# A two-layer attention and SwiGLU trunk on one core: another start of the attention phase, and other numbers in its planner

## The chip, the core and the metric

The kernel runs on one core of a Trainium2 chip. The metric is the device time of one execution in microseconds (us). TensorE (PE) multiplies, VectorE (DVE), ScalarE (ACT) and GpSimd (POOL) do the rest, and SyncE (SP) issues most transfers.

## The reference, cut to what matters

Two layers; in each a mixing part and a SwiGLU part, both with a norm before and after. All is float32, with 512 tokens of 1024 features, head size 64, 4 differential heads and 8 forgetting (fox) heads.

```python
cos, sin = rotary_tables(positions, x.dtype)      # 8 frequencies
for l in range(DEPTH):
    h = rms_norm(x, attn_pre_g[l])
    qa, ka, va, qb, kb, vb, f_logit = jnp.split(h @ w_in[l], split_at, axis=-1)
    qa = partial_rotary(qa, cos, sin)             # first quarter of each head
    ka = partial_rotary(ka, cos, sin)
    oa = diff_attention(qa, ka, va, lam)          # softmax 1 - lam * softmax 2, times va
    oa = rms_norm(oa, diff_sub_g[l]) * (1.0 - lam_init)
    log_f = jax.nn.log_sigmoid(f_logit + forget_bias[l])
    ob = forgetting_attention(qb, kb, vb, log_f)  # logits plus c_i - c_k, c = cumsum(log_f)
    x = x + rms_norm(jnp.concatenate([oa, ob], -1) @ w_out[l], attn_post_g[l])
    h = rms_norm(x, ffn_pre_g[l])
    y = (jax.nn.silu(h @ w_gate[l]) * (h @ w_up[l])) @ w_down[l]
    x = x + rms_norm(y, ffn_post_g[l])
```

## The kernel before, in words

**Exactness.** Every float32 matrix is split into a high part in TensorE's rounded float32 format (`A.copy`, ScalarE) and the rest (`tensor_sub`, VectorE or GpSimd), and a product takes three matmuls: high by high, high by low, low by high. So each weight chunk of 512 KB costs a transfer on SP's queue, a cast and a subtraction ahead of its 24 matmuls. `load_w` (L247) does this for the feed-forward part, `load` (L629) for the attention part. There are two raw buffers ("wr") and three pairs of split ones ("w").

**Stages.** Layer 0's attention runs from 0 to about 268 us, its feed-forward part to 584 and its down projection and the next norm to 644, layer 1's attention to about 876 us, and the rest to the end at 1231. The feed-forward products run in the plain order of the program, and the framework places what is not pinned. Instructions that are pinned keep the order of the program on their engine.

**The attention phase is planned.** `Plan` (L71) is a list scheduler that runs while the program is built. Every step is an `Op` with an engine, an estimated duration, its dependencies, a key (lower goes first), buffers that it takes and gives back, and a latency until its result can be used (for transfers the flight). `run` (L98) keeps one clock for each engine and for SP's queue and picks what can start first, by key among those that are ready. The order that it finds is pinned on each engine. The chip's own times do not matter any more then: each engine is in order, and an operation that comes later than planned holds up all behind it on its engine. Projections have the key `FILLER` (1e6): they go wherever TensorE has nothing else, in the fixed sequence `FILL = "d0 d1 d2 v1 d3 f0 v0 f1 f2 f3"`, and then the first part of the output projection (`o0_chunk`, L1090, columns 0 to 511 of w_out, and `o1_chunks`). Durations stand in `dV`, `dA` and `dG` (a fixed part and one for each column), and some are written at the place.

**A head.** A diff projection ("pj_kd", "pj_qd", `tile_chunk`, L670) gives a tile in PSUM. VectorE makes the rotary part: `t1` = tile * cosT, `pair` shuffles into `t2`, `t2` *= sinT (L739), `t1` += `t2`. `stack` splits the result by halves; for a key, SP copies each half to the other 64 partitions (`dup`, L714). Scores (`score`, L853) go to PSUM, VectorE adds the mask or the fox bias and takes the maximum (L875), ScalarE takes the exponential with its sum (L886). Diff heads then combine two rows ("ed", L958), fox heads scale one ("ae", L1037). TensorE transposes them, ScalarE and VectorE split them ("pth", "ptl", L919 and L923), and TensorE multiplies with V. GpSimd makes the fox bias ("ae", L1020 and L1022) from "cb", a row of sums that SP spreads over the partitions, and, in this kernel, the low parts of most weight chunks (L649).

**The start** (`start`, L397, layer 0 alone). x, the identity and four chunks of the diff V weights are loaded in turn, tokens are normalised by tiles of 128, transposed by TensorE ("hp_a") and split (L497, L502), and V is made tile by tile ("va"). Until then TensorE does empty products ("va<-sinT"). Raw V weights lie in `mixed_d` and `raw_v`, their split parts in the tiles of queries and keys. The rotary tables are made in `tables` (L525): eight transfers of positions, a chain of small VectorE steps (L554 to L572) behind the weights, three sines, a store to DRAM and four loads into cosT and sinT.

**The first gate chunks.** `gate` and `up` (L1229, L1232) call `proj_T` (L320). Its matmuls are pinned while `pinned[0]` holds, the splits of its weights are not.

Of the kernel before, what the change touches and what calls it, by code (L numbers as in the profile page):

```python
# [35 lines left out]
TB = S // 16  # L36
VA_C, VA_T = 4, 1
# [7 lines left out]
C_ID, C_M, C_F, NKEEP, C_U = 0, 128, 640, 641, 641  # L45
# [16 lines left out]
class Op:  # L62
    def __init__(self, eng, dur, fn, deps, key, take, give, lat):
        self.eng, self.dur, self.fn, self.key, self.take, self.give, self.lat = eng, dur, fn, key, take, give, lat
        self.users, self.after, self.left, self.ready, self.end = [], [], 0, 0.0, None
        for d in deps:
            d.users.append(self)
            self.left += 1


class Plan:  # L71


    def __init__(self, slots, margin):
        self.free = {k: [0.0] * n for k, n in slots.items()}
        self.margin, self.ops, self.last, self.idle = margin, [], {}, None

    def add(self, eng, dur, fn, deps=(), key=0.0, take=(), give=(), lat=0.0, order="", ready=0.0):
        o = Op(eng, dur, fn, deps, key, take, give, lat)
# [18 lines left out]
    def run(self, pin, first):  # L98
        clock = dict.fromkeys("VAGQ", 0.0)
        clock["P"] = first  # L100
        cands = {e: [o for o in self.ops if o.eng == e and not o.left] for e in clock}
        todo = len(self.ops)
        while todo:
            best = None
            for e, c in cands.items():
                opts = []
                for o in c:
                    s = self.slots_at(o)
                    if s is not None:
                        r = max(s, o.ready)  # L110
                        opts.append((max(r, clock[e]), o.key, r, o))
# [12 lines left out]
            clock[o.eng] = start + o.dur  # L124
            o.end = start + o.dur + o.lat
# [34 lines left out]
def _constants():  # L160
# [6 lines left out]
    c[:, C_M + S - P:C_M + S] = np.where(r[None, :] > r[:, None], np.float32(-BIG), np.float32(0.0))  # L167
    expo = np.arange(0, ROT, 2, dtype=np.float32) / np.float32(ROT)
    inv_freq = (np.float32(1.0) / np.power(np.float32(500000.0), expo).astype(np.float32)).astype(np.float32)
    c[:, C_F] = inv_freq[r // 16]  # L170
    return c
# [3 lines left out]
def hymba_block(ctx, tc, x_d, pos_d, apre_d, win_d, fb_d, lq1_d, lk1_d, lq2_d, lk2_d, dsg_d, wout_d, apost_d,  # L175
# [64 lines left out]
    V.memset(sinT, 0.0)  # L240
    G.memset(cosT, 1.0)
# [5 lines left out]
    def load_w(src, shape, name, eng=None, dst=None, raw=None):  # L247
# [10 lines left out]
        A.copy(hi, raw)  # L258
        (eng or V).tensor_sub(lo, raw, hi.bitcast(F32))  # L259
# [60 lines left out]
    def proj_T(src_w, col, name):  # L320

        wh, wl = load_w(src_w[:, col:col + P].rearrange("(k p) n -> p k n", p=P), [P, KT, P], name)
# [24 lines left out]
    for l in range(DEPTH):  # L347
        win = win_d[l]
        with ExitStack() as actx:
# [12 lines left out]
            mixed_d = ap.tile([P, NDIFF, S], F32, name=f"mixd{l}", tag="v8", bufs=5)  # L362
            if l == 0:
                raw_v = ap.tile([P, NDIFF, S], F32, name=f"rawv{l}", tag="v8", bufs=5)
# [18 lines left out]
            vd, tab = [], []  # L383
# [12 lines left out]

            def start():  # L397

                plan.free.update(g=[], v8=[0.0], qs=[], ks=[])
# [9 lines left out]
                idd = dma(con[:, :P], con_d[:, :P], P)  # L409

                def w_load(c):
                    raw = (mixed_d, raw_v)[c // 2][:, 2 * (c % 2):2 * (c % 2) + 2]
                    if c == 0:
                        dst = q_tile("wva0h"), q_tile("wva0l")
                    elif c < 3:
                        w = k_tile(f"wva{c}")
                        dst = w[:, 0], w[:, 1]
                    else:
                        dst = [wpool.tile([P, WCH], F32R, name=f"{x}_va3", tag=x).rearrange("p (a b) -> p a b", a=2)
                               for x in ("wh", "wl")]  # L420
                    hi, lo = dst
                    d = dma(raw, win[2 * c * P:(2 * c + 2) * P, VA:VA + S].rearrange("(k p) n -> p k n", p=P), 2 * S)
                    ops = []
                    for k in range(2):
                        wva[2 * c + k] = hi[:, k], lo[:, k]
                        a = add("A", dA(S), lambda k=k: A.copy(hi[:, k], raw[:, k]), [d], key=-85 + c,
                                take=["w"] if c == 3 and k == 0 else [], order="hi w" if c == 3 and k == 0 else "")
# [13 lines left out]
                zeros = sinT.bitcast(mybir.dt.bfloat16)  # L441
# [16 lines left out]
                for t in range(NT):  # L458
# [24 lines left out]
                    for z in range(2):  # L483
# [20 lines left out]
                        p = add("P", 436, tr, [v, idd], key=key, take=["ts"[z]], give=["e"])  # L504
# [3 lines left out]
                for t in range(NT):  # L508
                    for c in range(4):
                        def vas(t=t, c=c):  # L510
                            if t == NT - 1:
# [4 lines left out]
                                         key=500 + VA_C * c + VA_T * t)  # L516
                    vd_split(t, [done[t, 3]])
                for c in range(4):
                    add("P", 0, lambda: None, [done[t, c] for t in range(NT)], key=-99,
                        give=(["qs", "qs"], ["ks"], ["ks"], ["w"])[c])  # L520
                add("P", 0, lambda: None, wl[2] + wl[3], key=-99, give=["v8"])
                add("P", 0, first_va.clear, [done[t, 0] for t in range(NT)], key=-99)
                return hT[NT - 1, 1]

            def tables(last):  # L525

# [3 lines left out]
                tab_d = dpool.tile([4, 8, S], F32, name="tab_d", tag="tabd")  # L530
# [4 lines left out]
                def get(dst, src, n, **kw):  # L535
                    return add("Q", max(400, 1.43 * n), lambda: nc.sync.dma_start(dst(), src), key=1, lat=2000,
                               order="ld" + "".join(f" {k}" for k in kw.get("take", ())), **kw)

                def positions():
                    w = rbuf("rd", F32, "rot")  # L540
                    x["p"] = w[:, :TB].bitcast(I32)
# [901 lines left out]
```

## Time and profile before

| what | value |
| --- | --- |
| median of 3 runs | 1233.08 us (1230.33 to 1235.37) |
| the profiled execution's own time | 1233.1 us |
| its span, first to last instruction | 1231.3 us |
| busy: PE, DVE, ACT, POOL | 1195.3, 816.5, 597.1, 214.1 us |
| mean granted TensorE clock | 0.996 |

The span is the time that the trace shows; the execution's own time is 1.8 us longer. A matmul counts as busy from its start to its modelled end, so bare time of PE is the least that is lost. A name such as `t2kd<-t2kd,sinT` gives the tile that is written and those that are read.

### The profile page before, as it was taken

The numbers are of one execution on the slowest core, as the hardware profiler recorded it, in microseconds if no ns is written. First come the engines' busy times: TensorE is split into PE (matmuls) and PEld (weight loads), VectorE is DVE, ScalarE is ACT, GpSimd is POOL, SyncE is SP. The second block draws the span as 40 slices with busy tenths as digits, with TensorE's granted clock in tenths as the row PEclk, the third lists the DMA queues.
The fourth block names the chain that finished last, engine by engine and source line by source line (L and its number), as shares of the span: only waits on it lengthen the run. The fifth ranks groups of instructions, "written<-read, shape, count | busy, mean of one in ns | idle before, by whom it ended". The sixth has DMA issues, their size and how long they took to land.

```text
span 1231.3 us, 16721 instructions
## 1 busy us (share of the span) xinstructions
PE 1195.3 (97%) x5817; PEld 987.0 (80%) x5817; DVE 816.5 (66%) x1574; ACT 597.1 (48%) x1158; POOL 214.1 (17%) x250
## 2 busy tenths in 40 slices
PE   8998999999999999999999999999999999999997
PEld 5787877788888888888777878777988888888886
DVE  7698858765554555577848987695656455455776
ACT  5476657553332323365644767674533332333643
POOL 1302457320000000000223124672200000000010
PEclk9999999999999999999999999999999999999999
DMA  7333433416576676798513333433167667677964
GB/s 234 88 91 88 119 99 110 151 35 195 182 235 197 210 229 192 234 321 297 187 32 98 95 91 97 124 104 118 52 201 225 206 202 237 182 238 239 312 231 137
DMA packets 211268, 206.75 MB, mean 168 GB/s; under 512 B 11680, under 2 KB 155680, under 8 KB 211184
## 3 DMA queue, kind: packets, MB, share of 16 engines
q1 hardware_dynamic: 211040, 205.16, 53.5%
q8 instruction: 46, 0.75, 0.2%
q10 hardware_dynamic: 144, 0.52, 0.1%
q14 instruction: 38, 0.31, 0.1%
HBM read 163.34 MB, written 33.91 MB: 160 GB/s over the span
## 4 chain that ended last, share of the span: by engine, by line
PE 76%; DVE 11%; issue 7%; ACT 3%; POOL 2%; DMA 1%; POOLq 0%; DVEq 0%; SPq 0%; ACTq 0%
PE pj_g L205 20%; PE pj_u L205 19%; PE o L205 5%; PE da L205 5%; PE dc L205 5%; PE va L205 3%; PE pj_kd L205 3%; PE pj_kf L205 2%; PE db L205 2%; PE pj_qf L205 2%; PE vb L205 1%; DVE t2kd L739 1%; PE of L205 1%; PE pj_qd L205 1%; PE ptf L210 1%
## 5 line engine op out<-in xcount | busy, mean ns | idle before, releaser
L205 PE MATMUL pj_g<-hT_h,wh_g 128*128 128x512 f32 (+1 forms) x384 | 142.9, 372 | 0.0
L205 PE MATMUL pj_g<-hT_h,wl_g 128*128 128x512 f32 (+1 forms) x384 | 142.6, 371 | 0.0
L205 PE MATMUL pj_g<-hT_l,wh_g 128*128 128x512 f32 (+1 forms) x384 | 142.6, 371 | 0.0
L205 PE MATMUL pj_u<-hT_h,wh_u 128*128 128x512 f32 (+1 forms) x368 | 140.1, 381 | 0.0
L205 PE MATMUL pj_u<-hT_l,wh_u 128*128 128x512 f32 (+1 forms) x368 | 139.8, 380 | 0.0
L205 PE MATMUL pj_u<-hT_h,wl_u 128*128 128x512 f32 (+1 forms) x368 | 139.7, 380 | 0.0
L271 POOL TENSOR_SCALAR v_fp<-s_fp 128x1 f32<-128x1 f32 x8 | 7.6, 946 | 664.4 <-DVE c L1369 625.1
L259 DVE TENSOR_TENSOR wl_u<-wr_u,wh_u 128x1024 fp32r<-128x1024 f32 x44 | 53.9, 1225 | 99.6 <-ACT wh_u L258 99.6
L258 ACT CAST wh_g<-wr_g 128x1024 fp32r<-128x1024 f32 x44 | 46.4, 1054 | 146.3 <-PE pj_u L205 99.0
L258 ACT CAST wh_u<-wr_u 128x1024 fp32r<-128x1024 f32 x44 | 46.3, 1053 | 135.5 <-PE pj_g L205 128.3
L1239 DVE TENSOR_TENSOR sg<-pj_u,sg 128x512 f32<-128x512 f32 x44 | 30.4, 691 | 84.6 <-PE pj_u L205 84.6
L205 PE MATMUL da<-wh_d,op 128*128 128x512 f32 x264 | 82.6, 390 | 0.0
L205 PEld LDWEIGHTS pj_g<-hT_h,wh_g 128*128 128x128 f32 x384 | 72.3, 188 | 12.5
L205 PEld LDWEIGHTS pj_g<-hT_l,wh_g 128*128 128x128 f32 x384 | 72.3, 188 | 12.6
L205 PEld LDWEIGHTS pj_g<-hT_h,wl_g 128*128 128x128 f32 x384 | 72.3, 188 | 12.5
L205 PEld LDWEIGHTS pj_u<-hT_l,wh_u 128*128 128x128 f32 x368 | 69.2, 188 | 13.1
L205 PEld LDWEIGHTS pj_u<-hT_h,wl_u 128*128 128x128 f32 x368 | 69.2, 188 | 13.1
L205 PEld LDWEIGHTS pj_u<-hT_h,wh_u 128*128 128x128 f32 x368 | 69.2, 188 | 13.0
L258 ACT CAST wh_d<-wr_d 128x1024 fp32r<-128x1024 f32 x42 | 44.2, 1053 | 43.6 <-PE da L205 8.9
L259 DVE TENSOR_TENSOR wl_d<-wr_d,wh_d 128x1024 fp32r<-128x1024 f32 x42 | 51.3, 1221 | 17.7 <-ACT wh_d L258 17.5
L258 ACT CAST wh_d<-xr 128x1024 fp32r<-128x1024 f32 (+1 forms) x42 | 38.1, 908 | 43.7 <-PE da L205 13.2
L205 PEld LDWEIGHTS da<-wh_d,op 128*128 128x128 f32 x264 | 49.6, 188 | 10.2
(298 smaller groups left out, 3085.4 us busy)
## 6 DMA issues: line engine op xcount, KB each, us to landing
wr_g<-in_w_gate_dram SPq DMA_DIRECT2D x44, 512.0 KB, 4.6
wr_u<-in_w_up_dram SPq DMA_DIRECT2D x44, 512.0 KB, 4.6
b<-in_w_down_dram SPq DMA_DIRECT2D x88, 256.0 KB, 3.3
t_d<-b SPq DMA_DIRECT2D x88, 256.0 KB, 4.2
wr_d<-t_d SPq DMA_DIRECT2D x24, 512.0 KB, 4.6
wr_d<-in_w_down_dram SPq DMA_DIRECT2D x18, 512.0 KB, 5.0
wr_o<-in_w_out_dram SPq DMA_DIRECT2D x16, 512.0 KB, 4.4
xr<-t_d SPq DMA_DIRECT2D x16, 512.0 KB, 4.8
```

Source lines behind the costliest of these rows:

```text
L205: ins = PE.matmul(out, a, b, start=start, stop=stop)
L210: ins = PE.transpose(out, a, idn)
L258: A.copy(hi, raw)
L259: (eng or V).tensor_sub(lo, raw, hi.bitcast(F32))
L271: G.tensor_scalar(v, s2[:, 0:1], scalar1=s2[:, 1:2], scalar2=EPS, op0=ALU.add, op1=ALU.add)
L739: return V.tensor_mul(b["t2"], b["t2"], sinT)
L1239: V.tensor_mul(sg, pu, sg)
```

## The change

The start is another one. Raw V weights lie in the buffers of the probabilities ("pt"), their split parts in three tiles of "v8" and one pair of "w"; `mixed_d` is taken later (`mix`). The rotary tables are made at the very start (`rotary`): ScalarE loads the trigonometric table set and issues one transfer of the positions, with tokens on partitions; VectorE multiplies by eight constants and reduces the angle; ScalarE puts the sines into two zero or one tiles; TensorE transposes these in eight steps and ScalarE copies them to cosT and sinT. V products of token tiles 2 and 3 get a key behind the first diff projections, whose key goes ahead of other fillers. `Op` has a flag `port`: a flagged VectorE step does not start in the plan before the last GpSimd step has ended, and the reverse. Estimates are longer. The low parts of the `o0` chunks are made on VectorE instead of GpSimd. The splits of weight chunks are pinned where `proj_T` is called with `pinned[0]` set, which holds for the first four gate and up chunks of a layer.

```diff
+VA_C, VA_T, VA_EARLY = 4, 1, 2
...
+        self.port = port or eng == "G"
...
+        port = {"V": 0.0, "G": 0.0}
...
                         r = max(s, o.ready)
+                        if o.port:
+                            r = max(r, port["G" if e == "V" else "V"])
...
+            if o.port:
+                port[o.eng] = start + o.dur
...
-        A.copy(hi, raw)
-        (eng or V).tensor_sub(lo, raw, hi.bitcast(F32))
+        for ins in (A.copy(hi, raw), (eng or V).tensor_sub(lo, raw, hi.bitcast(F32))):
+            if pin:
+                tc.keep_in_program_order(ins)
...
             def dV(n):
-                return 68 + 1.04 * n
+                return 110 + 1.05 * n
             def dA(n):
-                return 60 + 0.83 * n
+                return 115 + 0.83 * n
             def dG(n):
-                return 120 + 2.15 * n
+                return 180 + 2.17 * n
...
+                tc.keep_in_program_order(A.preload_act_table_set("trig_and_small"))
...
-                                         key=500 + VA_C * c + VA_T * t)
+                                         key=(500 if t < VA_EARLY else FILLER - 20) + VA_C * c + VA_T * t)
...
+            def rotary():
+                key = -95
...
+                G.memset(tabs[0], 1.0)
+                G.memset(tabs[1], 0.0)
+                v = op("A", 500, lambda: A.dma_start(pos, pos_d[0].rearrange("(j p) -> p j", p=P)), [], lat=3000)
+                v = op("V", 80, lambda: V.tensor_copy(pf, pos), [v])
+                v = op("V", 700, lambda: [lambda f=f, c=c: V.tensor_scalar_mul(an[:, f * NT:(f + 1) * NT], pf, c)
+                                          for f, c in enumerate(_inv_freq())], [v])
...
+                    a = op("A", 800, lambda z=z: [place(z, half, m) for half in range(2) for m in range(2)], [dep])
...
+                    p = op("P", 436, tr, [a, idd[0]], take=["ts"[z]])
+                    ends.append(op("A", dA(S), lambda z=z: A.copy((cosT, sinT)[z], x[z]), [p], give=["ts"[z]]))
...
-                d = add("Q", 1.42 * n, raw, key=1e3, take=["wr"], lat=2000, order="ld")
+                d = add("Q", 1.42 * n, raw, key=1e3, take=["wr"], lat=2700, order="ld")
...
+                                       key=FILLER - 40 if kind == "d" and l == z == 0 else FILLER)
...
-                            e = add("Q", 730, dup(m), [e], key=key, lat=2000)
+                            e = add("Q", 730, dup(m), [e], key=key, lat=2700)
...
-                v3 = add("V", dV(S), t2, [v2], key=key)
+                v3 = add("V", dV(S), t2, [v2], key=key, port=True)
...
-                v = add("V", dV(n), top, [o], key=n_key, give=["s"])
-                return b, add("A", 282 + 0.83 * n, expo, [v], key=n_key)
+                v = add("V", dV(n)+80, top, [o], key=n_key, give=["s"])
+                return b, add("A", 370 + 0.87 * n, expo, [v], key=n_key)
...
-                cbd = add("Q", 730, cb_load, [st["c"]], key=n0 - 6, take=["rc"], lat=2000, order="rc")
+                cbd = add("Q", 730, cb_load, [st["c"]], key=n0 - 6, take=["rc"], lat=2900, order="rc")
...
-                    v = add("V", 75, inv, [a], key=nk)
-                    v = add("V", 70 + 0.65 * n, norm, [v], key=nk)
+                    v = add("V", 110, inv, [a], key=nk)
+                    v = add("V", 185 + 0.5 * n, norm, [v], key=nk, port=True)
...
                 box, ready = load(wout_d[l][kc * P:(kc + 2) * P, :S].rearrange("(k p) n -> p k n", p=P), [P, 2, S],
-                                  f"o0{l}{kc}")
+                                  f"o0{l}{kc}", eng=V)
```

The same flag stands on the diff combination, the low parts of rotary queries and keys and of every weight chunk, and on two steps of the diff norm.

## Rows read from the trace of the kernel before

**Rows 1.** Stages: length, busy us (instructions) of each engine, PEclk, DMA share, GB/s.

```profile
0.00:22.00 22.00, 18.17 (x78) 11.06 (x78) 13.50 (x23) 13.52 (x30) 5.62 (x16) 0.92 0.81 279
44.00:240.00 196.00, 185.93 (x1013) 152.39 (x1012) 162.23 (x423) 132.00 (x311) 82.33 (x87) 1.00 0.39 110
...
268.00:584.00 316.00, 316.00 (x1470) 264.77 (x1470) 183.82 (x267) 118.90 (x175) 2.20 (x4) 1.00 0.70 225
...
644.00:848.00 204.00, 192.17 (x1034) 158.21 (x1035) 164.92 (x426) 133.92 (x314) 84.76 (x88) 0.99 0.39 110
```

**Rows 2.** Waits of PE, 40 to 235 us: total us, times, longest.

```profile
PE ptf L210 <- DVE ae L1037: 1.7, 2, 1.1
...
PE o L205 <- DVE qsf L709: 0.9, 1, 0.9
PE ptd L210 <- DVE ed L958: 0.8, 1, 0.8
...
PE sd L205 <- issue: 0.7, 1, 0.7
```

**Rows 3.** Waits of PE, 644 to 848 us.

```profile
PE ptf L210 <- DVE ae L1037: 2.6, 2, 2.0
```

**Rows 4.** Timelines of POOL and DVE, 44 to 52 us: start, duration, instruction.

```profile
45.03 2.39 POOL L649 TENSOR_TENSOR wl_qd<-wr_qd,wh_qd 128x1024 fp32r<-128x1024 f32 x1 [2.82 <-ACT wh_qd L645]
...
45.47 2.50 DVE L739 TENSOR_TENSOR t2kd<-t2kd,sinT 128x512 f32<-128x512 f32 x1
```

**Rows 5.** Tiles t2kd (all) and ae (195 to 240 us) on DVE: min/median/max ns.

```profile
L739 DVE TENSOR_TENSOR t2kd<-t2kd,sinT x8: 686/2056/2505, 45.5 to 721.3; 128x512 f32<-128x512 f32 x8
...
L1037 DVE TENSOR_SCALAR ae<-ae,lf x15: 280/487/1720, 195.9 to 234.6; 128x256 f32<-128x256 f32 x4, 128x384 f32<-128x384 f32 x4, 128x512 f32<-128x512 f32 x4, 128x128 f32<-128x128 f32 x3
```

**Rows 6.** Groups by form on DVE, 44 to 240 us: busy us, mean ns | idle before.

```profile
L1037 DVE TENSOR_SCALAR ae<-ae,lf 128x128 f32<-128x128 f32 x8 | 3.6, 455 | 0.1
```

**Rows 7.** Chain that ended last, 205 to 240 us: start, us, what.

```profile
209.36 2.87 POOL wl_o L649
...
212.25 3.58 DMA wr_o<-in_w_out_dram
```

**Rows 8.** Timeline of DVE around 210 and 235 us.

```profile
210.17 3.13 DVE L649 TENSOR_TENSOR wo1l<-wr_o,wo1h 128x1024 fp32r<-128x1024 f32 x1 [0.22 <-ACT wo1h L645]
...
235.16 1.23 DVE L259 TENSOR_TENSOR wl_g<-wr_g,wh_g 128x1024 fp32r<-128x1024 f32 x1
```

**Rows 9.** DMA issues, 40 to 270 us: KB each, median us to landing.

```profile
wr_o<-in_w_out_dram SPq DMA_DIRECT2D x8, 512.0 KB, 4.4
ksd<-ksd SPq DMA_DIRECT2D x8, 256.0 KB, 3.4
...
cb<-cdram SPq DMA_DIRECT2D x8, 256.0 KB, 3.6
```

**Rows 10.** Timeline of DVE, 5 to 25 us.

```profile
6.21 0.69 DVE L472 CUSTOM_DVE_ANT_0 h_a<-xs 128x512 f32<-128x512 f32 x1 [4.83 <-DMA xs<-in_x_dram]
...
8.09 1.41 DVE L487 SCALAR_TENSOR_TENSOR h_a<-xs,r_s,g_apre 128x512 f32<-128x512 f32 x2 [1.18 <-POOL r_s L395]
...
24.36 0.68 DVE L428 TENSOR_TENSOR wl_va<-rawv,wh_va 128x512 fp32r<-128x512 f32 x1
```

**Rows 11.** Chain that ended last, whole span.

```profile
22.24 16.37 PE va L205 x72
38.61 5.45 PE pj_kd L205 x24
```

**Rows 12.** Tile rot, the tables' chain: min/median/max ns, first and last start.

```profile
L563 DVE SCALAR_TENSOR_TENSOR rot<-rot x9: 191/192/193, 28.3 to 31.0; 128x32 f32<-128x32 f32 x9
```

**Rows 13.** DMA issues, 0 to 30 us.

```profile
rot<-in_positions_dram SPq DMA_DIRECT2D x8, 2.0 KB, 5.3
...
dsg<-in_diff_sub_g_dram SPq DMA_DIRECT2D x2, 0.5 KB, 3.5
```

**Rows 14.** Timeline of DVE, 226 to 246 us: the last fox head's first and last step.

```profile
226.55 0.28 DVE L875 CUSTOM_DVE_ANT_0 ae<-sf,ae 128x128 f32<-128x128 f32 x1
...
241.20 0.69 DVE L1071 TENSOR_TENSOR hT_l<-mixf,hT_h 128x512 fp32r<-128x512 f32 x1 [0.69 <-ACT hT_h L1069]
```

More of the change, by code (lines that the diff above doesn't have):

```diff
@@ L76, in __init__, with add @@
         self.margin, self.ops, self.last, self.idle = margin, [], {}, None
-    def add(self, eng, dur, fn, deps=(), key=0.0, take=(), give=(), lat=0.0, order="", ready=0.0):
-        o = Op(eng, dur, fn, deps, key, take, give, lat)
+    def add(self, eng, dur, fn, deps=(), key=0.0, take=(), give=(), lat=0.0, order="", ready=0.0, port=False):
+        o = Op(eng, dur, fn, deps, key, take, give, lat, port)
         o.ready = ready
@@ L503, in start @@
                         v = add("V", 663, norm, [rd, gd], key=key, take=["e"] if SQ[z] == "A" else [])
-                        p = add("P", 436, tr, [v, idd], key=key, take=["ts"[z]], give=["e"])
+                        p = add("P", 436, tr, [v, idd[0]], key=key, take=["ts"[z]], give=["e"])
                         a = add("A", dA(S), hi, [p], key=key)
@@ L521, in start, with mix @@
-                add("P", 0, lambda: None, wl[2] + wl[3], key=-99, give=["v8"])
+                def mix():
+                    nonlocal mixed_d
+                    mixed_d = ap.tile([P, NDIFF, S], F32, name=f"mixd{l}", tag="v8", bufs=5)
+                add("P", 0, lambda: None, sum(wl.values(), []), key=-99, give=["pt", "pt"])
+                half, full = ([done[t, c] for t in range(NT)] for c in (1, 3))
+                add("P", 0, lambda: None, half, key=-99, give=["v8", "v8"])
+                add("P", 0, lambda: None, full, key=-99, give=["v8", "w"])
@@ L529, in tables @@
                 x = {}
-                tab_d = dpool.tile([4, 8, S], F32, name="tab_d", tag="tabd")
                 def op(eng, dur, fn, deps, **kw):
                     return add(eng, dur, fn, deps, key=key, **kw)
[L535 to L541, printed above, removed]
-                    x["a"], x["n"] = w[:, TB:2 * TB], w[:, 2 * TB:3 * TB]
-                    x["t"] = w[:, 4 * TB:8 * TB].rearrange("p (x j) -> p x j", x=4)
-                    blocks = pos_d[0].rearrange("(b j) -> b j", j=TB)
-                    return [lambda f=f: nc.sync.dma_start(x["p"][16 * f:16 * f + 16], blocks) for f in range(8)]
@@ L547, in sums @@
                 def sums():
                     x["tu"] = rbuf("rc", F32, "tu")
-                    return x["tu"]
-                dp = add("Q", 3000, positions, key=1, lat=2000, order="ld rd", take=["rd"])
-                dc = get(lambda: con[:, P:], con_d[:, P:NKEEP], S)
-                du = get(sums, con_d[:, C_U:C_U + S], S, take=["rc"])
-                v = op("V", 100, lambda: V.tensor_copy(x["a"], x["p"]), [dp])
-                v = op("V", 100, lambda: V.tensor_scalar_mul(x["a"], x["a"], con[:, C_F:C_F + 1]), [v, dc])
@@ L581, in tables @@
+                tab.append(add("Q", 1.43 * S, lambda: nc.sync.dma_start(con[:, P:], con_d[:, P:NKEEP]), key=1, lat=2000,
+                               order="ld"))
+                du = add("Q", 1.43 * S, sums, key=1, lat=2000, order="ld rc", take=["rc"])
+                p = op("A", 1300, lambda: A.preload_act_table_set("natural_log_exp_and_others"), last + tab)
                 tab.append(p)
@@ L687, in piece @@
                     return fn
-                last_tile[:] = fillers([(650, piece(k)) for k in range(KT)], [ready], take={0: ["g"]}, give=["w"])
+                last_tile[:] = fillers([(650, piece(k)) for k in range(KT)], [ready], take={0: ["g"]}, give=["w"],
+                                       key=FILLER - 40 if kind == "d" and l == z == 0 else FILLER)
                 done = last_tile[-1]
@@ L1002, in diff_head @@
                     mixed_d[:, h], mixed_d[:, h], dsg[:, l:l + 1], b["nrm"], op0=ALU.mult, op1=ALU.mult), [a, c],
-                    key=key + LAG_SS, give=["e"])]
+                    key=key + LAG_SS, give=["e"], port=True)]
             def fox_head(hh, n0):
```

137 lines of the change are left out of this document (72 added, 65 removed).

## The prediction

> **What bounds the kernel now.** I read the table of stages first. The feed-forward stretch from 268 to 584 us has TensorE busy for 316.00 of 316.00 us: nothing that this change touches can shorten it. The two attention phases are not full. From 44 to 240 us (layer 0) TensorE is busy for 185.93 of 196 us, from 644 to 848 us (layer 1) for 192.17 of 204, so 10.1 and 11.8 us are bare; the same rows have VectorE at 162.23 and 164.92 us, which is no bound but leaves little room [rows 1]. The work of TensorE stays, so a gain has to come out of these 21.9 us and out of the first 22 us.
>
> Second, the waits of TensorE. In layer 0 the longest are a transpose behind the normalised fox probabilities ("ae", 1.7 us in two waits), an output projection behind the query split ("qsf", 0.9), a transpose behind the diff combination ("ed", 0.8) and the first scores ("sd", 0.7, put down to issue) [rows 2]. Layer 1 has them again within 0.1 us, but 2.6 us for "ae" [rows 3]. The order was fixed by the planner, so each is an operation that came later than planned.
>
> Third, why it came later. At 45.47 us a product of two SBUF tiles on VectorE (t2kd) takes 2.50 us; a GpSimd split runs from 45.03 for 2.39 us and both end together [rows 4]. Undisturbed the product takes 686 ns, but its median is 2056; the scaling of a fox row of 128 columns takes 280 ns at least [rows 5] and 455 on average [rows 6]. Both planners give the two engines separate clocks, and the old one knows nothing of this. The held time in these two groups alone is about 4 x 1.4 + 32 x 0.18 = 11 us of VectorE a layer (an estimate: median less shortest, and the 128-column excess for all 32 scalings).
>
> **The change part by part,** against the profiled run's own 1233.1 us (span 1231.3; the median of the three runs is 1233.08, so nothing is to be corrected).
>
> *Port flags.* The plan now starts a flagged VectorE operation only after the last planned GpSimd one and the reverse. It removes no instruction; a hold that is foreseen gets a projection put into it. The waits behind it are "ae" and "ed": 1.7 + 0.8 in layer 0 and 2.6 + 0.8 in layer 1, 5.9 us [rows 2, 3]. Ends: nothing (actual times drift from planned ones) and 5.9. I take **-4.5**, nearer the upper, since the rows show the hold as the direct cause.
>
> *Splits of the first half of w_out go from GpSimd to VectorE.* Four chunks a layer. On GpSimd one holds the chain for 2.87 us, and the next weight transfer (3.58 us) starts only behind it [rows 7]. On VectorE such a split takes 1.23 us alone, but 3.13 when GpSimd is in one [rows 8]. So 4 x 2.87 = 11.5 us leave GpSimd and 4 x 1.23 = 4.9 us come to VectorE, where score evictions and probability splits queue behind them; its 34 us of room in layer 0 [rows 1] take that. The "qsf" wait follows that 3.13 us split; it goes if the split takes 1.23 us: 0.9 us in layer 0, nearly as much in layer 1. Ends: -1.7, and +4.9 a layer if every moved split stood on the path, which the room speaks against. I take **-1.5**.
>
> *Longer latencies.* Issue and flight of a key copy are planned at 730 + 2000 = 2730 ns and now 3430; the trace has 3.4 us. A row of sums goes from 2730 to 3630 against 3.6, a weight chunk from 3454 to 4154 against 4.4 [rows 9]. The first scores stand behind the key copy: 0.7 us in each layer [rows 2]. TensorE's waits name neither of the others, so they give nothing by themselves. **-1.4**, between 0 and -1.4; what a longer latency can cost is the second rival.
>
> *Longer durations of evictions, exponentials and splits.* What is left of the bare time is 10.1 - 4.1 us and 11.8 - 4.9 us, 12.9 together, in waits of about 1 us and less. Ends 0 and -12.9. With VectorE busy for 83% of the phase [rows 1] most of it will only move; I take a quarter, **-3.2**.
>
> *Clock.* The granted clock was 0.99 in layer 1's phase and 1.00 in layer 0's [rows 1]: 0.01 x 204 = 2.0 us, behind the one 2 us wait [rows 3]. It goes if that wait goes: **-1.0**, between 0 and -2.
>
> *The start.* V products of the last two token tiles are put behind the first diff projections, and the rotary tables are made first instead of behind the weight splits. VectorE sat idle for 4.83 us before x and 1.18 us before the norm, but was nearly full from 8.09 us to the last value split at 24.36 [rows 10]. The table chain is one cast, eight small products and 17 operations of about 0.2 us; nine of the present chain's steps took 191 ns each [rows 12]. At 0.22 a step that is 5.7 us on VectorE, ahead of the norms by key. Positions come through ScalarE's queue, behind a table load and the gain rows, in 512 runs of 4 bytes. Present positions landed after 5.3 us, a gain of one float for each partition after 3.5 [rows 13]; with issue at about 2 us I expect them at 6 to 7 us, so a third of the chain falls into idle time and the normalised tokens come 3 us later, at 28. TensorE ran its 72 last V products densely from 22.24 us [rows 11], 227 ns each, so by 24.4 it had done 24 + 10 of 96; by 28 it can have done the 48 of the first two tiles, 14 x 0.227 = 3.2 us more. That nearly pays for the delay. The eight added transposes cost 0.9 us (the plan's figure, 436 ns for four; they fall where TensorE waits anyway). **+1.0**; ends -2 (positions early) and +5 (VectorE held until they land). The removed table load and the DRAM round trip lay beside dense TensorE work and give nothing.
>
> A rule speaks against this: the Trainium skill, "DMA: Bandwidth & Descriptors", section "Rules for kernel authors", says that a strided last dimension lowers to one descriptor for each element and should be made contiguous. By it the new load is slower than the old one; the nearest row, 3.5 us for 128 runs of 4 bytes, does not bear that out so far, and no row has 512. What it would do is the third rival.
>
> *Earlier first head.* Its key projection ran from 38.61 us [rows 11]; it can now start near 30, as soon as two V banks are split. Spread over the phase this may fill later gaps: 0, with an end at -5.
>
> *Pinned splits.* At 235.16 us a 1.23 us split of the first gate chunk stands between the last heads' probability splits [rows 8]; pinned, it comes behind them. TensorE has output projections to do there: 0, between -1.2 and +1 a layer.
>
> **Sum:** 1233.1 - 4.5 - 1.5 - 1.4 - 3.2 - 1.0 + 1.0 = **1222.5 us.**
>
> **Rivals.**
> *The waits move* (chance 0.20). VectorE's in-order queue has 83% to do; whatever is put ahead of one wait is late for another. For it: the waits are many and short. Against: the holds are work time lost, not order. Only the 3 us of key copies and the query split stay, less 1 for the start: 1231.
>
> *Fillers run out* (0.17), the slower side. Longer planned latencies let the planner put more projections ahead of head work. They are a fixed stock; each used early is missing at the end. The last head takes from 226.55 to 241.9 us on VectorE [rows 14], 15.3 us, of which its own scores, transposes and products fill some 4; output projections fill the rest. If the stock ends half a head earlier, 5.7 us a layer are bare. It decides once the last head is the only work left. Against: the output projections come last in the stock anyway. 1233.1 + 11.4 + 1 - 4.5 = 1241.
>
> *Late tables* (0.12). Positions land at 10 us (issue at 2 and half as long again as now): VectorE, in order, holds the first norm from 8.09 to 12, and the rest of the chain adds 3.5: 7.4 us, of which the 3.2 us of V products are covered, so the start costs 4.2 instead of 1: 1226. The DMA rule named above would do this.
>
> *Deeper gain* (0.13). The earlier head (-5), half of the remaining 9.7 us of bare time and the rest of the clock (-1) also come: 1222.5 - 5 - 4.9 - 1 = 1212.
>
> *The forecast* itself has 0.38, with 1216 to 1227 as its own range.
>
> **Numbers.** About 0.5% (6.2 us) is what a measurement of this kernel can tell from no change: faster means below 1226.9, slower above 1239.3. Faster: 0.38 + 0.13 + half of the late tables = 0.57; same: 0.20 + 0.06 = 0.26; slower: 0.17. One in ten is left out at each end: low inside the deeper case, 1207; high at the middle of the slower one, 1241.
>
> **What would show it.** Right: TensorE's bare time in both attention phases at some 6 us; t2kd's median near 0.7 us; the "qsf" wait gone; scores no longer waiting for the first key copy; granted clock 1.00 in layer 1; the first key projection near 30 us. Wrong: the same bare time behind other names (waits moved); a gap after the last head's scores (fillers); the first norm after 11 us (late tables). If held VectorE products remain as they are and the time falls all the same, my main term is wrong.

## The result and the profile after

The changed kernel takes 1245.22 us (median of 4 runs, 1243.88 to 1246.37); the kernel before took 1233.93 in the same session (4 runs, 1230.33 to 1235.37). The ratio is 1.0093, with a 95% interval of 1.0077 to 1.0108: slower by 11.3 us. The prediction, 1222.5 us and a range up to 1241, was wrong. The profiled execution took 1243.88 us, its span is 1242.1 and its mean granted clock 0.988 (before 0.996).

The table of stages of the kernel after, with the columns of [rows 1]:

```profile
0.00:22.00 22.00, 17.04 (x71) 10.28 (x72) 14.60 (x46) 13.79 (x34) 5.66 (x17) 0.92 0.72 242
44.00:240.00 196.00, 189.45 (x1041) 160.08 (x1040) 154.27 (x421) 131.43 (x311) 74.85 (x83) 0.99 0.38 108
262.00:276.00 14.00, 5.92 (x31) 5.10 (x30) 8.22 (x11) 4.13 (x9) 2.68 (x6) 0.76 0.37 111
650.00:855.00 205.00, 194.96 (x1061) 164.40 (x1061) 160.65 (x429) 132.50 (x313) 75.65 (x84) 0.99 0.37 107
877.00:891.00 14.00, 5.94 (x33) 5.46 (x33) 8.14 (x11) 4.06 (x9) 2.06 (x4) 0.76 0.44 135
```

Read against [rows 1], the attention phases did what was hoped: TensorE is bare for 6.6 us instead of 10.1 in layer 0, and for 10.0 instead of 11.8 in layer 1. By the starts on TensorE the last output projection of layer 0 comes 4.7 us earlier (262.6 against 267.2 us), and layer 1's phase, from its first key projection to its last output projection, is 5.4 us shorter (225.8 against 231.2). The loss is where the prediction had looked for nothing, behind each attention phase: from 262 and from 877 us TensorE is busy for 5.9 of 14 us, and the mean granted clock is 0.76. In the kernel before it was busy for all of 14.00 us in both windows; its row for the first:

```profile
262.00:276.00 14.00, 14.00 (x102) 13.06 (x101) 10.62 (x18) 6.02 (x16) 4.28 (x8) 1.00 0.18 58
```

From the last output projection to the first down projection the kernel after takes 10.9 and 10.4 us longer in the two layers (253.3 and 252.7 against 242.4 and 242.3). So 10.1 us were won and 21.3 lost, which is the 11 us of the result. The waits of TensorE from 255 to 285 us in the kernel after (total us, times, longest):

```profile
PE pj_g L214 <- ACT wh_g L266: 6.2, 1, 6.2
PE pj_g L214 <- DVE wl_g L266: 2.3, 2, 1.9
```

ScalarE's and then VectorE's timeline there (start, duration, instruction):

```profile
267.44 0.63 ACT L286 ACTIVATE junk<-xs 128x512 f32<-128x512 f32 x1
...
268.07 1.03 ACT L266 CAST wh_g<-wr_g 128x1024 fp32r<-128x1024 f32 x1
269.00 1.04 ACT L266 CAST wh_u<-wr_u 128x1024 fp32r<-128x1024 f32 x1
...
277.96 1.05 ACT L266 CAST wh_g<-wr_g 128x1024 fp32r<-128x1024 f32 x1 [7.91 <-DMA wr_g<-in_w_gate_dram]
```

```profile
270.57 1.22 DVE L266 TENSOR_TENSOR wl_g<-wr_g,wh_g 128x1024 fp32r<-128x1024 f32 x1
271.70 1.22 DVE L266 TENSOR_TENSOR wl_u<-wr_u,wh_u 128x1024 fp32r<-128x1024 f32 x1
```

The first gate chunk's cast starts at 268.07 us, right behind the squares of the last token tile's pre-norm. The last output projection starts at 262.6 us, and the gate products wait for this cast (6.2 us) and then for the chunk's low half (1.9). The same cast in the kernel before, on ScalarE's timeline:

```profile
234.07 1.05 ACT L258 CAST wh_g<-wr_g 128x1024 fp32r<-128x1024 f32 x1
```

There it ran 34 us earlier, between the last heads' work; [rows 8] have the low half at 235.16. `keep_in_program_order` holds an instruction at the place where the program writes it, and proj_T is called behind the norms of all four token tiles. So the pin did not merely move the split behind the probability splits: it moved it behind the whole output stage. The third chunk comes late too: ScalarE is idle for 7.91 us behind the second cast, until that chunk's load has landed.

The signs that the prediction named, in the kernel after. First the waits of TensorE from 44 to 240 us, then from 650 to 855:

```profile
PE sd L214 <- DVE md L904: 2.4, 2, 2.0
PE ptf L219 <- DVE ae L1067: 1.3, 1, 1.3
PE o L214 <- DVE qsf L738: 0.8, 1, 0.8
PE ptd L219 <- DVE ed L987: 0.7, 2, 0.5
...
PE sd L214 <- DMA ksd<-ksd: 0.4, 1, 0.4
```

```profile
PE pj_kd L214 <- DVE vf L824: 3.3, 1, 3.3
PE o L214 <- DVE qsf L738: 1.3, 1, 1.3
PE ptf L219 <- DVE ae L1067: 1.1, 2, 0.9
```

The tile t2kd on VectorE, with the columns of [rows 5]:

```profile
L768 DVE TENSOR_TENSOR t2kd<-t2kd,sinT x8: 680/685/2502, 40.3 to 730.0; 128x512 f32<-128x512 f32 x8
```

Timelines of GpSimd at 96 us, of VectorE at 97 and 711 us and at the start, and of TensorE at the first key projection:

```profile
96.41 2.36 POOL L678 TENSOR_TENSOR wl_kf<-wr_kf,wh_kf 128x1024 fp32r<-128x1024 f32 x1 [1.62 <-ACT wh_kf L674]
...
97.29 1.50 DVE L979 TENSOR_TENSOR ld<-ld,nlam 128x1 f32<-128x1 f32 x1
...
711.89 1.65 DVE L979 TENSOR_TENSOR ld<-ld,nlam 128x1 f32<-128x1 f32 x1
...
6.91 0.17 DVE L560 CAST rot<-rot 128x4 f32<-128x4 int32 x1
...
8.24 0.75 DVE L502 SCALAR_TENSOR_TENSOR h_a<-xs,r_s,g_apre 128x512 f32<-128x512 f32 x1 [0.25 <-POOL r_s L406]
...
33.25 0.39 PE L214 MATMUL pj_kd<-hT_h,wh_kd 128*128 128x512 f32 x1
```

The load of the positions, among the DMA issues up to 30 us (KB each, us to landing):

```profile
rot<-in_positions_dram ACTq DMA_DIRECT2D x1, 2.0 KB, 5.3
```

Against [rows 2, 3] the "ae" waits shrank (1.7 to 1.3, 2.6 to 1.1), the "qsf" wait stayed (0.9 to 0.8; 0.8 to 1.3 in layer 1), and two have grown: 2.0 us near 97 us behind "md", as long as the longest before, and 3.3 us near 711 behind "vf". In front of both stands a small product (L979, 128x1) that is held on VectorE while a GpSimd split runs (from 96.41 and from 711.16 us): it takes 1.50 and 1.65 us, and 0.16 at the median. The "vf" wait is not new. The kernel before has it in both layers:

```profile
PE pj_kd L205 <- DVE vf L795: 1.1, 1, 1.1
```

t2kd's median fell from 2056 to 685 ns [rows 5], with two of the eight products still held, the first of each layer (2.47 and 2.50 us).

### The profile page after: what moved, and what is told of

Read it like the earlier page. It is cut to its first block, busy times and chain, and to the rows that moved or that the text cites. A ratio compares the mean times of both kernels' runs of the same rounds, so it can differ in the third digit from the quotient of the medians.

```text
span 1242.1 us, 16743 instructions
## 1 busy us (share of the span) xinstructions
PE 1194.2 (96%) x5826; PEld 994.1 (80%) x5826; DVE 809.5 (65%) x1588; ACT 598.4 (48%) x1164; POOL 194.9 (16%) x243
## 4 chain that ended last, share of the span: by engine, by line
PE 82%; issue 6%; DVE 6%; POOL 2%; ACT 1%; DMA 1%; POOLq 0%; DVEq 0%; SPq 0%; ACTq 0%
PE pj_g L214 19%; PE pj_u L214 19%; PE da L214 5%; PE dc L214 5%; PE pj_qd L214 4%; PE pj_kd L214 4%; PE pj_kf L214 4%; PE o L214 3%; PE vb L214 3%; PE pj_qf L214 3%; PE db L214 2%; PE va L214 2%; PE of L214 2%; PE sf L214 2%; PE ptf L219 1%
## 5 line engine op out<-in xcount | busy, mean ns | idle before, releaser
L214 PEld LDWEIGHTS pj_u<-hT_h,wl_u 128*128 128x128 f32 x368 | 69.2, 188 | 13.1
L266 DVE TENSOR_TENSOR wl_g<-wr_g,wh_g 128x1024 fp32r<-128x1024 f32 x44 | 53.7, 1220 | 14.7 <-ACT wh_g L266 13.5
```

The source lines that it names most:

```text
L214: ins = PE.matmul(out, a, b, start=start, stop=stop)
L266: for ins in (A.copy(hi, raw), (eng or V).tensor_sub(lo, raw, hi.bitcast(F32))):
```

## The experiments

Their sessions had the kernel before at 1234.2 to 1235.1 us, so differences of 1 us between sessions mean nothing.

**e1: the change without the pin.** In proj_T:

```diff
-        wh, wl = load_w(..., [P, KT, P], name, pin=pinned[0])
+        wh, wl = load_w(..., [P, KT, P], name)
```

> The changed kernel without the pins on the splits of the first gate and up chunks. Theory (the pins are the whole loss): the bare 6.2 and 1.9 us of TensorE before the first gate products and the half clock behind them go in both layers, some 10.5 us a layer, so about 1223 us, and the attention phases stay as short as in the changed kernel. Rival (the chunks come late for another reason, their transfers or the buffers that the new plan frees later): the gap stays, 1240 us or more.

Measured: 1229.35 us (7 runs), ratio 0.9955 (0.9938 to 0.9972), some 6 us above what was expected. The gap is gone:

```profile
262.00:276.00 14.00, 14.00 (x114) 13.69 (x113) 8.56 (x14) 5.08 (x13) 2.93 (x6) 1.00 0.23 77
```

From the last output projection to the first down projection the trace has 242.3 us in both layers, against 253.3 and 252.7 in the kernel after: the late pin costs 11.0 and 10.4 us there. Between the medians it is 15.9 us, in the main because the attention phases did not stay as short as expected: without the pin they are 1.1 and 2.9 us longer (first key projection to last output projection).

**e2: the kernel before with the pin alone.** The same `pin` argument put into the load_w and proj_T of before.

> The kernel before with the pins alone. Theory: the same gap of 8 us opens before the first gate products of both layers, with the same half clock, 1233 + 21 = 1254 us. Rival (the pins hurt only after the new plan): within 3 us of the kernel before.

Measured: 1258.62 us (4 runs), ratio 1.0190 (1.0170 to 1.0210), more than expected. The gap has the same shape. Waits of TensorE from 268 to 290 us, and the stage row:

```profile
PE pj_g L205 <- ACT wh_g L258: 6.6, 1, 6.6
PE pj_g L205 <- DVE wl_g L258: 2.2, 2, 1.9
```

```profile
270.00:284.00 14.00, 5.53 (x24) 4.57 (x23) 8.57 (x12) 5.41 (x13) 2.58 (x6) 0.66 0.26 87
```

By the starts on TensorE the output projections are followed 11.5 and 10.8 us later than before by the down projections; most of the rest lies in the attention phases, which are 3.6 and 1.5 us longer by this profile under the same plan. Why, no run shows. The pin needs nothing else of the change to do its harm.

**e3: the pinned splits written early.** The loads and splits of the first gate and up chunk are written ahead of all calls of o_norm, the second gate chunk's behind the last products of the output's first half; proj_T takes them ready-made:

```diff
+            w_g0 = proj_w(wg_d[l], 0, f"g{l}0")
+            w_u0 = proj_w(wu_d[l], 0, f"u{l}0")
...
+            w_g1 = proj_w(wg_d[l], ORDER[1] * P, f"g{l}{ORDER[1]}")
             o1.append(bank_s(f"o1{l}2"))
...
-            (g0, g0_part), (u0, u0_part), (g1, g1_part) = gate(0), up(0), gate(f1)
+            (g0, g0_part), (u0, u0_part), (g1, g1_part) = gate(0, w_g0), up(0, w_u0), gate(f1, w_g1)
```

> The changed kernel with the splits of the first three gate and up chunks pinned, but written ahead of the norms of the output projection (the first two) and behind its last chunk (the third). Theory (not pinning but the place in the program that the pin holds costs the time): no gap, 1221 to 1226 us. Rival (any pin there costs, by the order that it forces on ScalarE and VectorE): more than half of the loss stays, above 1234 us.

Measured: 1225.53 us (4 runs), ratio 0.9928 (0.9909 to 0.9947). All pins stand, and there is no gap. ScalarE's first gate cast, and the stage row:

```profile
241.11 1.05 ACT L266 CAST wh_g<-wr_g 128x1024 fp32r<-128x1024 f32 x1
```

```profile
262.00:276.00 14.00, 13.67 (x114) 13.33 (x113) 8.23 (x13) 5.90 (x13) 3.42 (x6) 1.00 0.25 79
```

So it is the place of the pinned split and not the pin: 19.7 us between one place and the other. The loads moved with the splits, but they were not what was late: in e1 they stand where the change has them, and there is no gap. e3 is the base of all runs below but e4.

**e4: the gap filled.** The kernel after, with 28 products of a constant tile into the waiting bank ahead of the first gate product (their results are overwritten):

```diff
+            for _ in range(28):
+                mm(g0, upr[:, :P], upr, True, True)
             g0_part(h0)
```

> The changed kernel with 28 empty products of 512 columns (6.4 us) ahead of the first gate products of each layer; their result is overwritten. The wait for the split weights is left. Theory (a part of the loss is TensorE's clock after the gap): the granted clock stays at 1.00 there, and 6.8 us at half clock give back 3.4 us a layer, so about 1237 us. Rival (the clock is no part of it): 1244 us or more.

Measured: 1243.80 us (4 runs), ratio 1.0072 (1.0056 to 1.0088). A miss: the clock in the gap was 1.00 in layer 0 and 0.88 in layer 1, yet the time hardly fell.

```profile
262.00:276.00 14.00, 11.81 (x70) 10.20 (x69) 8.53 (x12) 4.61 (x9) 2.60 (x5) 1.00 0.38 123
876.00:890.00 14.00, 11.82 (x59) 10.30 (x58) 8.22 (x11) 4.02 (x8) 2.14 (x5) 0.88 0.43 129
```

The first down projection of layer 0 comes 514.4 - 262.4 = 252.0 us behind the last output projection instead of 253.3; in layer 1, where a part of the gap stayed at the lower clock, it comes after 252.9 instead of 252.7. So the half clock costs some 1.3 us in layer 0. It could hardly cost more, since TensorE had little to do in the first 4 us of its stretch in the kernel after:

```profile
267.80:271.80 4.00, 0.80 (x2) 0.50 (x2) 2.56 (x4) 2.24 (x4) 0.86 (x2) 0.51 0.29 113
```

The loss is the wait.

**e5: no flags.** In e3's planner, `if o.port:` becomes `if False:`.

> Base: the version with the pinned splits placed ahead of the pre-norm, 1225.5 us. Here the plan no longer keeps flagged VectorE operations and GpSimd's apart; all else stays. Theory A (the flags carry the largest term of the forecast, 4.5 us): about 1230, and the time that VectorE's operations are held behind GpSimd's, 14.2 and 16.6 us in the two attention stretches, goes back towards the 21.5 and 22.2 us of the kernel before. Theory B (the flags do little for the time, because what they keep apart in the plan meets on the chip anyway, and the gain comes from the latencies, the splits on VectorE and the earlier start): 1225 to 1227.

Measured: 1238.65 us (6 runs), ratio 1.0025 (1.0011 to 1.0039): 13.1 us more than e3, above both theories. The flags do take holds away: from 44 to 240 us VectorE is busy for 159.7 us here and for 154.2 in e3, with nearly the same instructions (424 and 422).

**e6: the splits of the first half of w_out on GpSimd.** In o0_chunk of e3:

```diff
-                                  f"o0{l}{kc}", eng=V)
+                                  f"o0{l}{kc}")
```

> Base 1225.5 us. The splits of the first half of the output weights go back from VectorE to GpSimd; pins stay early. Forecast's term: 1.5 us of gain from having them on VectorE, so about 1227 here, with more operations of VectorE held behind the longer GpSimd splits in the last third of each attention stretch. Rival: the splits were hidden on GpSimd, 1225 to 1226. Other rival: VectorE gets 4 splits less per layer to do and the time falls, 1222 to 1224.

Measured: 1241.08 us (4 runs), ratio 1.0055 (1.0040 to 1.0070): 15.6 us more than e3, and above all three expectations. Its waits of TensorE from 205 to 228 us, then GpSimd's and VectorE's timelines there:

```profile
PE ptf L219 <- DVE ae L1070: 4.6, 2, 3.0
PE ptf L219 <- DVE ptlf L955: 3.0, 2, 2.4
```

```profile
215.49 2.35 POOL L681 TENSOR_TENSOR wo1l<-wr_o,wo1h 128x1024 fp32r<-128x1024 f32 x1
217.80 2.53 POOL L681 TENSOR_TENSOR wl_o<-wr_o,wh_o 128x1024 fp32r<-128x1024 f32 x1
...
217.34 5.23 DVE L1070 TENSOR_SCALAR ae<-ae,lf 128x512 f32<-128x512 f32 x5
```

Two splits stand back to back on GpSimd, and VectorE's five scalings take 5.23 us beside them.

**e9: both undone.** The edits of e5 and e6 together.

> Base: the version with the pinned splits placed early, 1225.5 us. Both the flags and the splits on VectorE undone at once: the plan keeps nothing apart, and the first half of the output weights is split on GpSimd as in the kernel before. One alone cost 13.1 us (no flags) and 15.6 us (GpSimd). Theory A (each costs on its own): the sum, about 1254. Theory B (the two only work together: a GpSimd split of 2.4 us is dear because flagged VectorE operations are planned behind all of it; without flags it does not matter who splits): 1236 to 1241, as without the flags alone. The forecast's own two terms would make it 1231.5.

Measured: 1229.66 us (4 runs), ratio 0.9954 (0.9937 to 0.9971). Neither theory: undone together they cost 4.1 us, where each alone costs 13 to 16. The three runs' stage rows for layer 0, e5 first:

```profile
44.00:240.00 196.00, 186.57 (x1021) 157.07 (x1020) 159.72 (x424) 133.83 (x313) 74.97 (x83) 0.98 0.39 108
```

e6:

```profile
44.00:240.00 196.00, 181.89 (x990) 153.39 (x988) 154.09 (x415) 129.38 (x307) 82.86 (x87) 0.97 0.38 107
```

e9:

```profile
44.00:240.00 196.00, 189.25 (x1031) 159.41 (x1030) 156.70 (x420) 133.46 (x313) 81.53 (x87) 0.98 0.39 107
```

TensorE is bare for 9.4, 14.1 and 6.8 us, against 6.2 in e3. By these runs the flags and the moved splits are one term, and half of it is worse than none. For e6 the rows name the wait. For e5 no single wait stands out, and since changed planned numbers alone moved the time by 8 to 10 us (e7, e8), a part of the 13 and 16 us can be the luck of the order that was dealt.

**e7, e10: the planned latencies.** Both on e3: 2700, 2700 and 2900 ns become 2000 each (e7), or 2350, 2350 and 2450 (e10).

```diff
-                d = add("Q", 1.42 * n, raw, key=1e3, take=["wr"], lat=2700, order="ld")
+                d = add("Q", 1.42 * n, raw, key=1e3, take=["wr"], lat=2000, order="ld")
```

> Base 1225.5 us. The plan's latencies of weight chunks, key copies and rows of sums go back from 2700, 2700 and 2900 ns to 2000 ns. Forecast's term: 1.4 us of gain from the longer ones, so about 1227 here, with waits of the first-half output products on their chunk or of scores on their key copy in the trace. Rival: the transfers were early enough either way, and the order moves at random: 1223 to 1228 with no new wait on a transfer.

> Base 1225.5 us with the planned latencies of 2700, 2700 and 2900 ns; 1217.5 us with 2000 ns for all three. Here 2350, 2350 and 2450 ns. Theory A (a longer planned latency by itself delays work in the plan): between the two, 1220 to 1223. Theory B (the 8 us are the luck of one order against another: a change of a planned time re-deals the order, and a few waits of 1 to 3.5 us appear or vanish with it): no order between the three; anything from 1215 to 1230, below 1217 or above 1226 being the sign of it.

Measured: e7 1217.45 us (4 runs), ratio 0.9862 (0.9847 to 0.9877), below all that was expected; e10 1226.93 (4 runs), 0.9936 (0.9919 to 0.9953). The middle values give no middle time, so the 8 us do not follow the size of the latency. The stage around 97 us, in e3 and in e7 (whose phase starts 1.5 us earlier):

```profile
92.00:112.00 20.00, 17.11 (x91) 13.28 (x90) 15.97 (x60) 16.73 (x48) 4.75 (x2) 0.91 0.26 71
```

e7:

```profile
90.00:110.00 20.00, 19.20 (x117) 15.97 (x116) 17.72 (x64) 17.67 (x45) 8.10 (x4) 1.00 0.31 81
```

e7 has 2.1 us more of TensorE busy there and no fall of the clock, which in e3 takes 0.09 x 20 = 1.8 us. e10 has e3's row again, clock 0.91.

**e11: the planned durations** of score evictions, exponentials, reciprocals and row scalings as before, on e3 (`dV(n)+80` to `dV(n)`, `370 + 0.87 * n` to `282 + 0.83 * n`, and so on).

> Base 1225.5 us. The planned durations of score evictions, exponentials, reciprocals and row scalings go back to the values of the kernel before; copies, tensor products and GpSimd's keep the new ones. Forecast's term for all longer durations: 3.2 us of gain, so about 1228.5 here. Rival (luck of the order, as with the latencies): anything from 1217 to 1235, with the difference in waits of 1 to 3.5 us behind VectorE that this change does not name.

Measured: 1225.49 us (4 runs), ratio 0.9920 (0.9900 to 0.9940): no difference from e3, where 3 us more were expected, though layer 0's phase became 2.9 us shorter (first key projection to last output projection) and layer 1's 2.8 us longer.

**e8, e13, e12: the small product with lambda.** e8 and e13 move it from VectorE to ScalarE. e8 also plans 120 ns less on VectorE and 200 more on ScalarE; e13 keeps every planned number, and with it the order; its edit is shown. e12 is e8 with e7's latencies.

```diff
-                                lambda: V.tensor_mul(b["r"][:, 1:2], b["r"][:, 1:2], nlam[:, l:l + 1])]
+                                lambda: A.activation(b["r"][:, 1:2], b["r"][:, 1:2], AF.Copy, scale=nlam[:, l:l + 1])]
```

> Base 1225.5 us. The 128x1 product of the reciprocals with lambda (two operands from SBUF, no flag in the plan, 32 in all) leaves VectorE for ScalarE, ahead of the scaling that reads it there; the plan counts 200 ns more on ScalarE and 120 ns less on VectorE. Theory: that product, held 1.50 us behind a GpSimd split, causes the new waits of TensorE at 97 us (2.19 us) and part of those near 700 us; they go, and 4.7 and 1.5 us less of VectorE's time is held: 1220 to 1223. Rival: ScalarE's 32 added instructions (some 0.2 us each) lie on the chain from scores to probabilities and take back as much, or the operations behind the removed one are held in its place: 1225 to 1228.

> Base 1225.5 us (pins early). The 128x1 product with lambda runs on ScalarE, all planned numbers unchanged, so TensorE, VectorE (less that product) and GpSimd keep their order. Theory A (the held product is the cause of the wait): the wait of 2.2 us near 97 us and the half clock after it (granted clock 0.91 in the 20 us around it, 1.8 us) go: about 1221.5. Theory B (the order was the cause, and what stands behind the held product is held in its place, or the wait is for something else): the wait at 97 us stays and the time is 1225 to 1227.

> Pins placed early, the product with lambda on ScalarE (alone 1215.5 us), and the three latencies back at 2000 ns (alone 1217.5 us). If the two gains were of separate causes they would add: 1207.5. If both only removed the same waits near 97 us of layer 0 (both took 5 us of layer 0's attention stretch, 229.2 to 224): 1212 to 1216.

Measured: e8 1215.46 us (4 runs), ratio 0.9847 (0.9832 to 0.9861); e13 1225.92 (4 runs), 0.9934 (0.9917 to 0.9950); e12 1215.73 (4 runs), 0.9844 (0.9830 to 0.9859). e8 came out lower than its theory said, and e13 overturned that theory. e13's GpSimd and VectorE near 97 us, and the waits of TensorE from 92 to 112 us:

```profile
95.83 2.48 POOL L681 TENSOR_TENSOR wl_kf<-wr_kf,wh_kf 128x1024 fp32r<-128x1024 f32 x1 [1.44 <-ACT wh_kf L677]
...
97.34 1.02 DVE L846 SCALAR_TENSOR_TENSOR az<-lg 128x32 f32<-128x32 f32 x1
```

```profile
PE sd L214 <- DVE md L907: 1.9, 2, 1.5
```

With the held product gone, the next unflagged operation is held in its place (1.02 us; 0.17 in the kernel after), and "md" is still late. e8 differs from e13 in its planned numbers (and in where ScalarE has the product), so what helped e8 is the new order that they dealt. e12 adds nothing to e8, as expected of two orders that lose the same waits. e8 and e12 beat both kernels of this case, by 1.5% against the one before.

**e14: V products not postponed** (on e3):

```diff
-VA_C, VA_T, VA_EARLY = 4, 1, 2
+VA_C, VA_T, VA_EARLY = 4, 1, 4
...
-                                       key=FILLER - 40 if kind == "d" and l == z == 0 else FILLER)
+                                       key=FILLER)
```

> Base 1225.5 us (pins early). The V products of the last two token tiles of layer 0 come before the first key projection again, and that projection's tile has the ordinary key; the tables stay early. The forecast's step had the normalised tokens 3 us late and 3.2 us of V products covering it: about 1228.5 if that holds. Rival (the first head's start 5 us earlier buys nothing, as the same products have to be done later): 1225 to 1226 with the first key projection near 38 us. Luck of the order can move either by 4 us; bare time of TensorE before 50 us tells the start apart from that: in the base it is 4.5 us up to 22 us and 0 from there to 50.

Measured: 1229.96 us (8 runs), ratio 0.9964 (0.9952 to 0.9977): 4.4 us more than e3. Its first key projection:

```profile
39.80 0.39 PE L214 MATMUL pj_kd<-hT_h,wh_kd 128*128 128x512 f32 x1
```

That is 7 us later than in e3 (32.8) and 1.4 later than before (38.4), so the early tables by themselves delay the first head by 1.4 us. But the sign that was named ahead, bare time of TensorE before 50 us, does not show the 4.4 us:

```profile
0.00:22.00 22.00, 17.74 (x74) 10.61 (x75) 14.79 (x47) 14.04 (x35) 5.67 (x17) 0.92 0.70 242
22.00:50.00 28.00, 28.00 (x132) 23.34 (x131) 15.20 (x31) 10.69 (x17) 4.80 (x2) 1.00 0.40 105
```

It is 4.3 us up to 22 us and none from there, in e3 4.5 and none. So the loss lies behind the start, in the order that was dealt: layer 0 now has a wait of 3.3 us behind "vf", which e3 has in layer 1 alone. The time came near the forecast's 1228.5, but not by the start; what the postponed products are worth is open.

## Why the prediction was wrong

**The step that failed is "Pinned splits", taken at 0, between -1.2 and +1 a layer.** It measured +11.0 and +10.4 us (e1). The step read the right row [rows 8], but asked only what the split would no longer disturb. It did not follow the pinned instruction to its place in the program. proj_T(g0) is written behind o_norm of the last token tile, so the cast waits for the squares, and these for the last output projection. "TensorE has output projections to do there" is just what fails: the split comes when the last of them is done. None of the rivals had this gap. What the step did have right is small: behind the last heads the splits no longer disturb them. With the pins placed early the phases are 1.2 and 3.1 us shorter than without pins (e3, e1).

**The sum of the other steps came out near, in part by luck.** Without the pin the change gives 1229.35 us, with the splits written early 1225.53, against a forecast of 1222.5 whose own range was 1216 to 1227. But the terms don't stand singly, and other planned numbers moved the sum by 8 to 10 us (e7, e8):

- *Port flags* -4.5 and *splits to VectorE* -1.5: together -4.1 on the chip (e9), alone nothing of the kind. Either without the other costs 13 to 16 us (e5, e6). The list of waits behind these terms left out "vf", 1.1 us in each layer and the second longest in layer 0, and this is the wait that grew to 3.3. The "qsf" wait stayed although the splits beside it run undisturbed now, since two of them stand ahead of the query split where there was one:

```profile
205.45 1.22 DVE L678 TENSOR_TENSOR wl_o<-wr_o,wh_o 128x1024 fp32r<-128x1024 f32 x1
206.59 1.22 DVE L678 TENSOR_TENSOR wo1l<-wr_o,wo1h 128x1024 fp32r<-128x1024 f32 x1
207.84 1.39 DVE L738 TENSOR_TENSOR qsf<-pj_qf,qsf 64x512 fp32r<-64x512 f32 x2
```

- *Longer latencies* -1.4: undoing them gained 8.1 us, going halfway nothing (e7, e10). Which order the plan deals weighs more than the latency. The two rivals that let longer estimates push the time one way ("the waits move", "fillers run out") had this wrong as well. The reason of the term was not in its row either: the first scores' 0.7 us [rows 2] are put down to issue, and the key copies, issued from 50.1 to 50.8 us and landed within 3.6 us, were there before TensorE went on to these scores at 56.3.
- *Longer durations* -3.2: nothing for four kinds of operation (e11). The longer times of copies and tensor products were not undone alone.
- *Clock* -1.0: no. It stayed at 0.99 in layer 1 and fell to 0.99 in layer 0, behind the new waits.
- *The start* +1.0: near, as far as two profiled executions tell. The tables were not late (cast at 6.91 us, first norm 8.24 against 8.09 [rows 10]), and the last split of tokens ends at 26.6 us against 24.4, 2.1 us later where 3 were expected. TensorE is bare for 1.1 us more up to 22 us (4.96 against 3.83) and for none from there to 50 in either kernel. No run shows what the postponed products give (e14).
- *Earlier first head* 0: the key projection came at 33.2, not near 30; what that is worth by itself is open.

**The signs.** Bare time near 6 us came true in layer 0 only, t2kd's median near 0.7 us too; the "qsf" wait stayed, the first scores wait 0.4 us for a key copy, the clock stayed at 0.99 in layer 1, and waits of 2.0 and 3.3 us took the place of the old. "The waits move" was thus half right as to mechanism.

*Late tables* did not happen: the load of 512 runs of 4 bytes landed after 5.3 us, as the one before had [rows 13]. The Trainium skill, "DMA: Bandwidth & Descriptors", section "Rules for kernel authors", says that a strided last dimension lowers to one descriptor for each element; at this size the trace shows no loss by it.

Of what remains of the gain without flags and moved splits (e9, 5.3 us), the parts of the start, the order and the early pins are open; they were not tried apart.

## What to carry to other kernels

Before an instruction is pinned to its program order, look up where the program writes it and what stands ahead of it there on its engine: a pin is a wait for all of that. Where a planner lists the order, a single planned number moves the time by as much as the effects one wants to give it (here by up to 10 us: e7, and e8 against e13), so a term of 1 to 5 us can't be read from one such run, and a candidate is best run with several dealt orders. Two edits that rest on each other (which operations are kept apart, and which engine does the long ones) are to be judged together.

## What the runs showed of the hardware

A product of one element for each partition is held behind GpSimd as a large one is: 1.50 us for 128x1 beside a 2.36 us split, with a median of 160 ns over its 32 executions in the kernel after, and in e13 1.02 us for 128x32. It ends with the split (98.79 and 98.77 us), while the 512-column product of [rows 4] ends 0.55 us behind its split (47.97 against 47.42), and not together with it as the prediction read. The Trainium skill, "GPSIMD Engine Reference", section "1. Specifications", says that GpSimd's SBUF interfaces are shared with VectorE, with contention for instructions of VectorE with two SBUF inputs; the held product has two, and the trace agrees. The times of one kernel's executions go with the mean granted clock: e1 took 1225.74 us at 0.995 and 1233.37 at 0.989. A wait of 2 us costs more than itself: the 20 us around the one at 97 us in e3 have a granted clock of 0.91, and in e7, without that wait, 1.00. And in e4 products without use kept the clock at 1.00 through layer 0's gap, which gave back only 1.3 us: in the kernel after TensorE was busy for 0.80 us of the first 4.00 at the lower level.
